# Sample keys turned by VectorE in 32x32 blocks and scored with 32x32-tile products

## The chip, the core and the metric

The kernel runs on one core of one Trainium2 chip. The metric is the device time of one execution in microseconds (us). Three runs of the kernel before took 1339.94, 1340.01 and 1341.91 us; the median is 1340.01 us.

## The reference, cut to what matters

The program is one inference step of a two-layer decoder: a short gated convolution layer and a native sparse attention (NSA) layer, each between two half-step SwiGLU networks, for 256 prompt tokens and 8 sequences of 4 new tokens ("samples"), model width 1024, 16 heads of 64 in 4 key/value groups, all in float32. The change is in the part of the NSA layer that attends from the sample tokens to their caches: a compressed branch, a selected branch (the 16 best of 32 blocks of 64 cached tokens) and a window branch (the last 512 cached tokens).

```python
s_s = jnp.einsum('bqkgd,bqkjld->bqkgjl', q, k_sel).astype(jnp.float32) * scale
s_s = jnp.where(m_s, s_s, NEG)
p_s = jax.nn.softmax(s_s.reshape(B, Tq, N_KV_HEADS, GROUP, n_sel * L_SEL), axis=-1)
o_s = jnp.einsum('bqkgjl,bqkjld->bqkgd', p_s.astype(q.dtype), v_sel)
...
s_w = jnp.einsum('bqkgd,bskd->bqkgs', q, kv_win[:, :, 0]).astype(jnp.float32) * scale
p_w = jax.nn.softmax(jnp.where(m_w, s_w, NEG), axis=-1)
o_w = jnp.einsum('bqkgs,bskd->bqkgd', p_w.astype(q.dtype), kv_win[:, :, 1])
```

The kernel does not gather blocks. It scores all 2048 cached tokens of a sequence and adds a large negative number to blocks that were not selected.

## The kernel before

The dense products (feed-forward networks, convolution, projections) run on TensorE (PE) as exact pairs: each weight is split into a high and a low part (`W.convert`: ScalarE copies, VectorE or GpSimd subtracts) and three products are added. They fill most of the execution and are not changed. Weights come through a ring of 4 buffers `raw` of 1 MB and a ring of 4 split pairs `whi`, `wlo`, in the order of a list; the SyncE queue (SP) issues their loads.

The NSA layer (`nsa`) first makes its projections: keys and values (6 blocks of 256 columns), gates, then the 8 query blocks `u`. A query block's prompt part goes to `qT`; its sample part goes to `Qbd`, a block-diagonal layout in which a sequence and a pair `pr` of key/value groups own 32 columns (2 groups x 4 tokens x 4 heads). Once all weights up to the attention have been loaded, `load_pages` starts to fill free `raw` buffers with cache pages; five more buffers, `page`, exist only from the attention on, since their pool (`att`) takes the room of a pool that the projections use (`tin`). A page is 512 tokens of one sequence, keys and values, 1 MB; each partition holds 4 tokens (index `s`). Window pages are loaded by SP, selected-branch pages by an indirect DMA on the GpSimd queue (POOL).

The attention then interleaves two streams by a hand-written order.

The samples: 4 pairs of sequences `i`, each with 5 chunks (window `w`, then 0 to 3) of one page for each of the two sequences, so 20 chunks `c`. For a chunk:

- `s_turn` (steps a and b, one for each sequence): PE transposes the page's keys, 8 transposes of 128x128 for each sequence; ACT copies 3 of the 4 resulting 128x512 PSUM tiles to SBUF, DVE the fourth, into the free split buffers.
- `s_scores` (step s): 4 products of K=128, 32 rows, 512 columns, in the four column tiles of the array, into one PSUM bank; DVE adds the mask, scales and takes the maximum in one instruction (line 1302), and ACT takes the exponential (line 1303).
- `s_turn_p` (step p): 4 transposes of the exponentials, copied by ACT to `PTs` (line 1316).
- `s_values` (step v): 16 products, 32 rows in the four column tiles; then the pages' buffers are free and `load_pages` issues the next loads.

Small steps for each pair (scores of compressed blocks and of new rows, ranking, weights of the branches, output) are hooked into the rounds.

The prompt: 8 units `u`, each of four items, `prompt_scores` twice (row half `kp` 0 and 1), `prompt_turn` (12 transposes and three copies to SBUF), `prompt_values`.

The order: `START = 'isabiiRiCS'` opens (i one prompt item, s the small scores, a and b the transposes, R the ranking, C a transpose for the prompt's compressed branch, S the scores of chunk 0). Then each round c runs `ROUND = 'abi0p1si2v'`: the transposes and scores of chunk c+1, the turn and values of chunk c, and 0.92 prompt items at each i as long as there are any, with a few kept for the last rounds. PE, DVE and ACT each take their instructions in the order in which the program puts them out; `soon` and `spend` keep an estimated clock, so that a step that hangs on another engine is put out later.

PSUM has 8 banks: in the attention 3 for scores (`mm`), 3 for transposes (`tr`), 2 for values (`acc`), each kind a ring.

Of the kernel before, what the change touches and what calls it, by code (L numbers as in the profile page):

```python
# [47 lines left out]
# the past blocks' compression beside the dense products: its share of the time, and what its loads take  # L48
# [11 lines left out]
KT_ACT, PT_ACT = (1, 2, 3), 1  # L60
# [84 lines left out]
def tile_step(ctx, tc, x_prompt, x_sample, state_conv, cache_cmp, cache_sel, cache_win, page_table,  # L145
# [33 lines left out]
    # ---- inputs wanted first  # L179
# [28 lines left out]
    # ---- constants  # L208
# [14 lines left out]
    # ---- the stream of weights  # L223
# [78 lines left out]
    # ---- the residual stream, transposed: [d, token]  # L302
# [54 lines left out]
    def begin(pg, pu):  # L357
        """The first products, each step as soon as its part of the input has been turned and split."""
# [66 lines left out]
    def products2(p0, p1, ah, al, late=2, between=None):  # L425
        """Two outputs at a phase's start: the inputs that come last are used last."""
# [182 lines left out]
    # ---- the last norm: turned as it comes, scaled when the tokens' factors are known  # L609
# [45 lines left out]
    # ---- the compressed branch's past blocks: they hang on the cache alone  # L655
# [8 lines left out]
    def indices():  # L664
        # a gathered row is two tokens of a block: partition (q, n) takes tokens 8 q + 2 i of block n
# [41 lines left out]
    def load_w1(pool):  # L707
        w = pool.tile([P, 16, P], F32, name="W1", bufs=1)
# [4 lines left out]
    def cmp_side(cw):  # L713
# [4 lines left out]
        # rows (q, d) and steps (i, l, h) of a block's token 8 q + 2 i + l and column 32 h + d  # L718
# [27 lines left out]
        # the first layer's share of the positions: a product with one column  # L746
# [53 lines left out]
    # ---- native sparse attention  # L800
    def nsa(at, v_next):
# [8 lines left out]
        def big(n, name):  # L810
            """A slot of the weights' split parts, free while attention runs."""
# [6 lines left out]
        W1 = load_w1(tin)  # L818

        # constants over rows r = (b2, pr, kp, t, g), tokens and blocks  # L820
# [48 lines left out]
        # a row's token is 4 * (b2 + 2 i) + t  # L869
# [7 lines left out]
        # new rows: of the row's own sequence, no later than its token  # L877
# [10 lines left out]
        # ---- projections  # L888
# [4 lines left out]
        nc.gpsimd.memset(Qbd, 0.0)  # L893
        R, V = {}, {}
# [7 lines left out]
        def rows(t, src, a):  # L902
            dst, dst_s, pb = outs[t]
            if a == 0:
                R[t] = T("Rk", [P, 2, 256])
                V[t // 2] = A(f"V{t}", [P, 2, 256]) if t else T("Rv", [P, 2, 256])
# [624 lines left out]
```

## Time and profile before

| | us |
|---|---|
| median of three runs | 1340.01 |
| span of the profiled execution (first to last instruction) | 1333.6 |
| attention stage in it, 918.65 to 1079.03 | 160.4 |
| PE busy in that stage | 153.4 |
| ACT busy in that stage | 110.5 |
| DVE busy in that stage | 94.2 |
| POOL busy in that stage | 49.5 |

The profile is of one execution. The own time of that execution is known only by its span; the runs' times also hold what lies around a span. In the profile's rows, PE is a matrix product, PEld a load of its stationary operand, DVE is VectorE, ACT ScalarE. A row of a group names the line, the engine, the operation, what is written and read, the shape, the count, then busy time and mean duration, then the idle time before with what ended it. A float32 product shows as two records. Products show the line of the helper that issues them (177, transposes 221), so their tiles tell them apart: `mm<-whi,Qbd` and `mm<-wlo,Qbd` are the sample scores, `tr<-ident,page` and `tr<-ident,raw` the key transposes, `acc<-page,PTs` and `acc<-raw,PTs` the sample values, `mm<-kT,qT` the prompt scores.

### The profile page before, as it was taken

The numbers are of one execution on the slowest core, as the hardware profiler recorded it, in microseconds if no ns is written. First come the engines' busy times: TensorE is split into PE (matmuls) and PEld (weight loads), VectorE is DVE, ScalarE is ACT, GpSimd is POOL, SyncE is SP. The second block draws the span as 40 slices with busy tenths as digits, with TensorE's granted clock in tenths as the row PEclk, the third lists the DMA queues.
The fourth block names the chain that finished last, engine by engine and source line by source line (L and its number), as shares of the span: only waits on it lengthen the run. The fifth ranks groups of instructions, "written<-read, shape, count | busy, mean of one in ns | idle before, by whom it ended". The sixth has DMA issues, their size and how long they took to land.

```text
span 1333.6 us, 26864 instructions
## 1 busy us (share of the span) xinstructions
PE 1309.6 (98%) x11009; PEld 1242.0 (93%) x11009; DVE 815.4 (61%) x1512; ACT 616.7 (46%) x1115; POOL 353.5 (27%) x356
## 2 busy tenths in 40 slices
PE   8999999999999999999999999999999999999997
PEld 8999999999999999999999999998776688999997
DVE  5675566677666555667655555666556456554553
ACT  5443444443454433345433445454766655443444
POOL 2331233243323222333321121303333123220211
PEclk9999999999999999999999999999999998999999
DMA  8767555756565575457656344765577964766432
GB/s 261 197 195 245 187 189 171 234 183 204 191 194 192 162 236 198 144 181 246 193 171 206 127 143 144 215 192 222 206 269 285 300 165 163 246 251 221 142 118 75
DMA packets 202893, 262.12 MB, mean 197 GB/s; under 512 B 14958, under 2 KB 188610, under 8 KB 197524
## 3 DMA queue, kind: packets, MB, share of 16 engines
q1 hardware_dynamic: 179792, 182.34, 43.5%
q0 software_dynamic: 14304, 75.61, 16.0%
q10 hardware_dynamic: 8676, 2.48, 1.0%
q8 instruction: 86, 1.41, 0.4%
q14 instruction: 35, 0.29, 0.1%
HBM read 257.38 MB, written 11.35 MB: 202 GB/s over the span
## 4 chain that ended last, share of the span: by engine, by line
PE 87%; DVE 6%; ACT 4%; issue 2%; POOL 1%; DMA 0%; ACTq 0%; SPq 0%; POOLq 0%; DVEq 0%
PE mm L177 74%; PE acc L177 8%; PE tr L221 4%; DVE wlo L117 2%; ACT whi L116 1%; DVE rt L739 1%; DMA rt<-in_x_prompt_dram 0%; ACT sq L332 0%; ACT wlo L1166 0%; ACT S L1166 0%; DVE xT L523 0%; ACT L527 0%; ACT whi L1280 0%; DVE xl L326 0%; POOL ue L542 0%
## 5 line engine op out<-in xcount | busy, mean ns | idle before, releaser
L177 PE MATMUL mm<-xh,whi 128*128 128x288 f32 x1832 | 548.5, 299 | 2.2 <-DVE xl L1215 0.9
L177 PE MATMUL mm<-xh,wlo 128*128 128x288 f32 x1832 | 544.1, 297 | 2.7 <-DVE wlo L117 1.7
L177 PE MATMUL mm<-xl,whi 128*128 128x288 f32 x1832 | 536.7, 293 | 1.1 <-DVE xl L326 1.1
L117 DVE TENSOR_TENSOR wlo<-raw,whi 128x1024 fp32r<-128x1024 f32 (+2 forms) x358 | 402.2, 1136 | 109.0 <-ACT whi L116 107.2
L116 ACT ACTIVATE whi<-raw 128x1024 fp32r<-128x1024 f32 (+2 forms) x365 | 343.1, 953 | 107.8 <-PE mm L177 90.7
L177 PEld LDWEIGHTS mm<-xh,whi 128*128 128x128 f32 x1832 | 344.8, 188 | 8.1 <-issue 3.9
L177 PEld LDWEIGHTS mm<-xl,whi 128*128 128x128 f32 x1832 | 349.1, 191 | 2.8 <-DVE xl L326 2.5
L177 PEld LDWEIGHTS mm<-xh,wlo 128*128 128x128 f32 x1832 | 344.2, 188 | 3.7 <-DVE wlo L117 2.4
L490 POOL TENSOR_TENSOR a<-s,t 128x288 f32<-128x288 f32 x88 | 111.9, 1271 | 445.8 <-DVE t L488 273.0
L177 PE MATMUL mm<-Ah,whi 128*128 128x288 f32 x768 | 229.4, 299 | 0.0
L177 PE MATMUL mm<-Ah,wlo 128*128 128x288 f32 x768 | 227.9, 297 | 0.7 <-DVE wlo L117 0.7
L177 PE MATMUL mm<-Al,whi 128*128 128x288 f32 x768 | 227.5, 296 | 0.0
L177 PEld LDWEIGHTS mm<-Ah,whi 128*128 128x128 f32 x768 | 145.2, 189 | 2.6 <-issue 1.9
L177 PEld LDWEIGHTS mm<-Ah,wlo 128*128 128x128 f32 x768 | 144.1, 188 | 1.4 <-DVE wlo L117 1.4
L177 PEld LDWEIGHTS mm<-Al,whi 128*128 128x128 f32 x768 | 144.4, 188 | 0.0
L486 ACT ACTIVATE s<-t 128x288 f32<-128x288 f32 x88 | 39.1, 445 | 172.4 <-DVE t L484 170.4
L733 POOL DMA_INDIRECT rc<-in_cache_cmp_kv_dram,idxc x64 | 70.8, 1107 | 134.2 <-DVE rt L739 117.0
L493 ACT ACTIVATE Ah<-a 128x288 fp32r<-128x288 f32 x88 | 39.2, 445 | 128.0 <-POOL a L490 127.7
L488 DVE TENSOR_TENSOR t<-mm,rB 128x288 f32<-128x288 f32 x88 | 39.9, 454 | 79.1 <-PE mm L177 79.1
L739 DVE STREAM_TRANSPOSE rt<-rc 128x1024 f32<-128x1024 f32 x64 | 78.3, 1233 | 9.2 <-PE acc L177 9.1
L494 DVE TENSOR_TENSOR Al<-a,Ah 128x288 fp32r<-128x288 f32 x88 | 40.0, 454 | 58.8 <-ACT Ah L493 58.8
L523 DVE SCALAR_TENSOR_TENSOR xT<-mm,xT 128x288 f32<-128x288 f32 x64 | 29.2, 456 | 71.2 <-PE mm L177 70.9
(348 smaller groups left out, 1249.3 us busy)
## 6 DMA issues: line engine op xcount, KB each, us to landing
raw<-in_w_ffb_gu_dram SPq DMA_DIRECT2D x44, 1024.0 KB
raw<-in_w_ffa_gu_dram SPq DMA_DIRECT2D x42, 1024.0 KB
raw<-in_w_ffa_down_dram SPq DMA_DIRECT2D x16, 768.0 KB
raw<-in_w_conv_in_dram SPq DMA_DIRECT2D x12, 1024.0 KB
raw<-in_w_ffb_down_dram SPq DMA_DIRECT2D x16, 768.0 KB
raw<-in_w_ffa_down_dram SPq DMA_DIRECT2D x16, 640.0 KB
raw<-in_w_ffb_down_dram SPq DMA_DIRECT2D x16, 640.0 KB
out_dram<-in_cache_win_kv_dram POOLq DMA_DIRECT2D x8, 1016.0 KB, 6.9
```

The costliest lines, as they stand in the source:

```text
L116: self.nc.scalar.activation(parts[0], v, AF.Copy)
L117: (lower or self.nc.vector).tensor_sub(parts[1], v, parts[0])
L177: nc.tensor.matmul(out, lhsT, rhs, start=start, stop=stop, skip_group_check=True)
L221: nc.tensor.transpose(out, in_, ident[:k, :k])
L486: nc.scalar.activation(s1, t1, AF.Silu)
L488: nc.vector.tensor_mul(t2, pu[:, :N], rB)
L490: nc.gpsimd.tensor_mul(a, s1, t2)
L493: nc.scalar.activation(Ah[:, f], a, AF.Copy)
L494: nc.vector.tensor_sub(Al[:, f], a, Ah[:, f])
L523: nc.vector.scalar_tensor_tensor(xT[:, d], py[:, :N], 0.5, xT[:, d], op0=OP.mult, op1=OP.add)
L733: nc.gpsimd.indirect_dma_start(out=tiles[i], out_offset=None, in_=rows_c, in_offset=bass.IndirectOffsetOnAxis(ap=idxc[:, i:i + 1], axis=0))
L739: nc.vector.transpose(turned[i], tiles.pop(i))
```

## The change

- `s_turn`: instead of 8 transposes on PE and two copies, one DVE instruction for each page transposes each 32x32 block of the keys in place (128 partitions x 4 x 256).
- A copy of the queries, `Qr`, repeats each 32-row piece of `Qbd` on all four 32-row groups, with zeros where the row of `Qbd` belongs to the other key/value group. `replicate` (step Q of START) makes it from 16 products with the identity and four copies, two on ACT, two on DVE. GpSimd clears it ahead.
- `s_scores`: 64 products of K=32, 32 rows, 128 columns, each in one of the 16 tiles of 32x32, four of them added up for one result; the four row groups write four different PSUM banks. The moving operand takes the four tokens of a partition as the inner index, 512 elements apart. The mask instruction reads the four banks at once, and the scores' order in SBUF becomes (token in page, s).
- `s_turn_p` reads the scores with four elements between neighbours.
- One PSUM tile `sc` of four banks holds the scores of samples and of the prompt; `tr` has two banks instead of three.
- `prompt_scores` handles one half of the queries at a time for both row halves `kp`, whose products follow each other in separate banks; all three copies of `prompt_turn` go to ACT.
- The five `page` buffers are allocated with the projections; two of them first hold `W1`, `XP` and two row buffers, and three are free for pages. Tiles that had room of their own (`S0`, `PB`, `PcT`) go to the split buffers and to `ss`.

```diff
-ATT = dict(mm=3, tr=3, acc=2)
+ATT = dict(tr=2, acc=2)
...
-START = 'isabiiRiCS'
+START = 'iQsabiiRiCS'
...
+        def page():
+            return at.tile([P, 2048], F32, name="page", bufs=PAGES)
+        W1 = load_w1(page())
+        XPR = page().rearrange("p (a x) -> p a x", a=4)
...
+        Qr = A("Qr", [P, NB * 2, 4, 32])
+        nc.gpsimd.memset(Qr, 0.0)
...
-        room = {"raw": 0, "page": 0}
+        room = {"raw": 0, "page": PAGES - 2}
...
             if W.loaded == W.stop:
-                room["raw"] = RAW - W.live - len(pages)
+                room["raw"] = RAW - W.live - sum(r == "raw" for r in rings.values())
                 load_pages()
+            else:
+                load_pages(True)
...
+        SC = banks["pool"].tile([P, 4, 512], F32, name="sc", bufs=1)
...
+        def replicate():
+            for c in range(4):
+                kp = c // 2
+                ps = accb()
+                cs = slice(c * 32, (c + 1) * 32)
+                for q4 in range(4):
+                    mm(ps[q4 * 32:(q4 + 1) * 32, :256], ident[cs, cs],
+                       Qbd[cs].rearrange("p b r x -> p (b r) x")[:, :, kp * 16:(kp + 1) * 16], True, True)
...
-        def prompt_scores(u, kp):
+        def prompt_scores(u, half):
...
+            b0 = 2 * (next(turns) % 2)
+            ps = [SC[:, b0], SC[:, b0 + 1]]
+            for br in range(2):
+                for kp in range(2):
+                    ks = slice(kp * 64, (kp + 1) * 64)
+                    mm(ps[kp][:, br * w:(br + 1) * w], qT[ks, u, qs], K[br + 1][ks, pr, :w], True, True)
...
         def s_turn(c, b2):
             i, j = chunks[c]
-            t = pages[i, j, b2]
-            KT[c, b2] = big(1024, ("whi", "wlo")[b2]).rearrange("p (a k) -> p a k", a=2)
-            for pr in range(2):
-                pt = trb()
-                for s in range(4):
-                    tr(pt[:, s * P:(s + 1) * P], t[:, s, pr * P:(pr + 1) * P])
...
+            k = pages[i, j, b2][:, :, :256]
+            nc.vector.transpose(k, k)
...
-            ps = mmb()
-            for q, b2, pr in groups():
-                mm(ps[q * 32:(q + 1) * 32], Qbd[:, 2 * i + b2, pr], KT[c, b2][:, pr], True, True)
...
+            for h in range(4):
+                kc = [slice(pr * P + h * 32, pr * P + (h + 1) * 32) for pr in range(2)]
+                for q4 in range(4):
+                    qs = slice(q4 * 32, (q4 + 1) * 32)
+                    for q, b2, pr in groups():
+                        mm(SC[q * 32:(q + 1) * 32, q4, :P], Qr[qs, 2 * (2 * i + b2) + pr, h],
+                           pages[i, j, b2][qs, :, kc[pr]].rearrange("p s x -> p x s"), h == 0, h == 3)
+            S = T("S", [P, P, 4], F32, 2)
```

More of the change, by code (lines that the diff above doesn't have):

```diff
@@ L59 @@
 HOOKS = ((-5, 1), (-3, 1), (3, 2), (4, 2), (5, 0), (5, 2))
-KT_ACT, PT_ACT = (1, 2, 3), 1
 EARLY = (2, 1)
@@ L928, in rows @@
                 nc.sync.dma_start(dst_s[0].rearrange("b t c k d -> (b t) (c k d)"), RS[pb:pb + NS])
-        XP = [T(f"XP{c}", [P, 16, KV, 8]) for c in range(2)]
+        XP = [XPR[:, c].rearrange("p (a k n) -> p a k n", k=KV, n=8) for c in range(2)]
         def cmp_prompt_in():
@@ L1035, in nsa, with load_pages @@
         pages, rings = {}, {}
-        room = {"raw": 0, "page": 0}
+        room = {"raw": 0, "page": PAGES - 2}
         done = []
-        def load_pages():
+        def load_pages(early=False):
             while len(pages) + len(done) < len(order):
-                ring = max(room, key=lambda r: room[r])
+                ring = "page" if early else max(room, key=lambda r: room[r])
                 if not room[ring]:
-                    return
+                    break
                 i, j, b2 = key = order[len(pages) + len(done)]
@@ L1046, in load_pages @@
                 room[ring] -= 1
-                t = raw.tile([P, 2048], F32, name="raw") if ring == "raw" else T("page", [P, 2048], F32, PAGES)
+                t = raw.tile([P, 2048], F32, name="raw") if ring == "raw" else page()
                 if j == "w":
@@ L1055, in load_pages @@
                 rings[key] = ring
-            W.stop, W.bufs = None, room["raw"]
-            W.load_ahead()
+            if not early and len(pages) + len(done) == len(order):
+                W.stop, W.bufs = None, room["raw"]
+                W.load_ahead()
         clock, due, ties = [0.0], [], count()
@@ L1148, in prompt_cmp2 @@
             nc.vector.tensor_copy(PcT, ps[:, :NP])
-        def prompt_scores(u, kp):
+        def prompt_scores(u, half):
             pr, g = divmod(u, 4)
-            if kp == 0:
-                units[u] = (big(4 * NP, ("whi", "wlo")[u % 2]).rearrange("p (j k) -> p j k", j=4), T("S0", [P, 4, P], F32, 2),
+            if half == 0:
+                units[u] = (big(4 * NP, ("whi", "wlo")[u % 2]).rearrange("p (j k) -> p j k", j=4), big(512, ("wlo", "whi")[u % 2]).rearrange("p (j k) -> p j k", j=4),
@@ L1169, in prompt_scores @@
+            if half:
                 soon(2.0, lambda: prompt_factor(u), ("u", u))
@@ L1437, in items @@
                 share[0] -= 1
-        room["page"] = PAGES
+        room["page"] += 2
         load_pages()
-        steps = dict(i=item, s=lambda: s_small(0), a=lambda: s_turn(0, 0), b=lambda: s_turn(0, 1), S=lambda: s_scores(0), R=lambda: s_rank(0), C=prompt_cmp2)
+        steps = dict(i=item, s=lambda: s_small(0), a=lambda: s_turn(0, 0), b=lambda: s_turn(0, 1), S=lambda: s_scores(0), R=lambda: s_rank(0), C=prompt_cmp2, Q=replicate)
         for step in START:
```

76 lines of the change are left out of this document (32 added, 44 removed).

## The prediction

> **What bounds the kernel now.** I read the page first, then the granted clock and busy times in stretches, then one round of the attention in the timeline, then the groups of instructions and the waits of that stage.
>
> ```profile
> span 1333.6 us, 26864 instructions
> PE 1309.6 (98%) x11009; PEld 1242.0 (93%) x11009; DVE 815.4 (61%) x1512; ACT 616.7 (46%) x1115; POOL 353.5 (27%) x356
> PE 87%; DVE 6%; ACT 4%; issue 2%; POOL 1%; DMA 0%; ACTq 0%; SPq 0%; POOLq 0%; DVEq 0%
> ```
>
> TensorE is the bound of the whole. The span is 1333.6 us, the median of the runs 1340.0, so 6.4 us lie around the span; I take it that this execution is like the median, work out a difference, and put it on 1340.0. The change touches only the attention stage (and some loads before it), so that stage decides. One round handles one chunk; the ACT copy of its turned scores (PTs, line 1316) marks it:
>
> ```profile
> 935.26 0.60 ACT L1316 ACTIVATE PTs<-tr 128x512 f32<-128x512 f32 x1
> 1024.83 0.62 ACT L1316 ACTIVATE PTs<-tr 128x512 f32<-128x512 f32 x1
> 1065.08 0.60 ACT L1316 ACTIVATE PTs<-tr 128x512 f32<-128x512 f32 x1 [0.25 <-PE tr L221]
> ```
>
> These are the 1st, 12th and 20th of the 20. They cut the stage, from the prompt's first scores to the output projection, into head, 11 rounds that also carry the prompt's items, 8 rounds almost without, and a drain (columns: stretch, its length, then busy time of PE, PEld, DVE, ACT and POOL, the clock granted, the DMA share and GB/s):
>
> ```profile
> 918.65:935.26 16.61, 15.65 (x124) 12.21 (x128) 13.34 (x69) 14.47 (x50) 5.29 (x4) 0.90 0.56 233
> 935.26:1024.83 89.57, 86.61 (x991) 62.21 (x993) 52.54 (x230) 62.02 (x196) 31.53 (x30) 1.00 0.66 244
> 1024.83:1065.08 40.25, 38.90 (x496) 27.96 (x491) 18.92 (x75) 24.11 (x58) 7.68 (x9) 1.00 0.98 324
> 1065.08:1079.03 13.95, 12.26 (x120) 8.82 (x120) 9.43 (x34) 9.88 (x28) 5.00 (x3) 1.00 0.79 146
> ```
>
> A mixed round lasts 89.57/11 = 8.14 us, a plain one 40.25/8 = 5.03. PE is busy 97% of both, DVE 59% and 47%. So PE sets the stage, and DVE has room: 37.0 us in the mixed rounds, 21.3 in the plain ones.
>
> **What leaves PE.** A round in full: its 16 key transposes, its four wide score products (two records each), its value products, and one item of prompt scores.
>
> ```profile
> 939.55 2.03 PE tr L221 x16
> 1017.81 0.96 PE mm L177 x8
> 1020.23 1.08 PE L177 MATMUL acc<-raw,PTs 128*32 128x128 f32 x32
> 1014.92 1.57 PE L177 MATMUL mm<-kT,qT 64*128 64x256 f32 x8
> ```
>
> The transposes go: 20 x 2.03 = 40.6 us of PE. The wide products go too: 20 x 0.96 = 19.2. Prompt scores now run the two row halves next to each other into separate banks; if they overlap, 8 items' worth of 1.57 is spared, 12.6 us at most, 0 at least; I take 10.
>
> **What comes to PE.** 64 products of 32x32 tiles a chunk, hence 128 records as each f32 product shows two. No row here has 32-row tiles side by side. The nearest rows bound it:
>
> ```profile
> 1017.50 0.31 PE L177 MATMUL acc<-kT,Qbd 128*32 128x32 f32 x16
> 1017.63 0.60 PE L177 MATMUL mm<-whi,Qbd 128*32 128x512 f32 x2
> 1018.06 0.60 PE L177 MATMUL mm<-whi,Qbd 128*32 128x512 f32 x2
> ```
>
> Sixteen records of four column tiles were put out between 1017.50 and 1017.63: 8.1 ns each. 128 x 8.1 = 1.04 us is the lower end, and some 0.2 us until the last one ends makes 1.25. The upper end is the value products, four column tiles abreast and the rows one after the other: 1.08/32 = 34 ns a record, 4.3 us a chunk. I take 1.25, nearer the lower end, because column tiles do run abreast here and the sixteen tiles are as independent. PE's work in the stage becomes 153.4 - 40.6 - 19.2 - 10 + 25 = 109 us: no longer the bound.
>
> [...] The new products read keys with 2 KB between neighbours, and the score transposes read S with 16 bytes between neighbours. No row before shows such a read; the price, if it binds, is worked out as a rival below. [...]
>
> Spreading the queries (16 products of 256 columns, four abreast) is 1.7 us of PE in the head: a wide product's second record starts 0.43 us after its first (1017.63, 1018.06), so 256 columns in two records take 0.43, four times. The head loses the transposes of two chunks, 4.1 us, against it.
>
> The score transposes' weight loads cost 0 more in my sum, and 0.56 us a round if they doubled (4 x 0.14); they lie beside DVE's work.
>
> **What comes to DVE, and what leaves it and ACT.**
>
> ```profile
> L739 DVE STREAM_TRANSPOSE rt<-rc x64: 1200/1236/1247, 75.7 to 745.8; 128x1024 f32<-128x1024 f32 x64
> L1282 DVE COPY whi<-tr 128x512 f32<-128x512 f32 x20 | 13.8, 688 | 8.5 <-PE tr L221 7.7 <-issue 0.8
> L1198 DVE COPY whi<-tr 128x512 f32<-128x512 f32 x4 | 2.8, 688 | 1.8 <-PE tr L221 1.8
> L1198 DVE COPY wlo<-tr 128x512 f32<-128x512 f32 x4 | 2.8, 688 | 1.6 <-PE tr L221 1.6
> L1280 ACT ACTIVATE wlo<-tr 128x512 f32<-128x512 f32 x40 | 22.2, 595 | 1.3 <-PE tr L221 1.3
> L1280 ACT ACTIVATE whi<-tr 128x512 f32<-128x512 f32 x20 | 11.8, 592 | 7.5 <-PE tr L221 7.3
> L1302 DVE CUSTOM_DVE_ANT_1 S<-mm,mk 128x512 f32<-128x512 f32 x16 | 11.0, 690 | 19.9 <-PE mm L177 19.9
> ```
>
> Two block transposes of 128x1024 a chunk: 2.47 us, 49.4 in all; in place and from four runs of 256 is not shown, and I price it the same. One copy of 0.69 a chunk goes (13.8), and the prompt's eight copies move to ACT (5.6). DVE in the stage: 94.2 + 49.4 - 19.4 + 0.8 (two of the four Qr copies at the 0.42 of a 128x256 group) = 125 us. ACT falls from 110.5 by 34.0 and gains 8 x 0.6 and 0.8: 82. DVE becomes the busiest engine.
>
> **The new wait.** Scores of samples and of the prompt now share one set of four banks (before: a ring of three). In a round DVE turns two pages, then PE can run the chunk's products, then DVE alone frees the banks (line 1302's 0.69). DVE's own queue stands still while PE works, 1.25 us a round, except for the small steps placed there (softmax factors, ranking); I take it half filled: 0.6. Behind DVE's waiting instruction stand the next chunk's transposes and the prompt's maxima, and PE waits for both. DVE's transposes also wait for the page, now at the head of DVE's queue rather than PE's:
>
> ```profile
> DMA to landing us min/median/max: 5.5/7.2/13.7
> ```
>
> Nine slots hold 4.5 chunks, so a page is asked for more than three rounds, 15 us, ahead: 0, at most a few us in the plain rounds where DMA already stands at 0.98.
>
> **The sum.** Mixed round on DVE: 52.54 busy - 11 x 0.69 - 5 x 0.69 (the prompt's copies) + 11 x 2.47 = 68.7, or 6.25 a round; + 0.6 = 6.85. Saved: 11 x (8.14 - 6.85) = 14.2 us. Plain round: (18.92 - 5.5 + 19.8)/8 = 4.15, + 0.8 (fewer small steps to fill with) = 4.95 against 5.03: saved 0.6. Head: 13.34 - 2.1 + 4.9 + 0.8 = 17 us of DVE in order plus its first waits, against 16.61: lost 2. Drain: one PE copy path against another, 0. Some rounds under the half clock (below): lost 3. Together -9.8: **1330 us**.
>
> **Edits at nothing.** The ring opening earlier: before, pages were issued from 900 on, and none held PE when the first transposes began.
>
> ```profile
> 900.03 1.02 POOL L1052 DMA_INDIRECT raw<-in_cache_sel_kv_dram,idxs  x1 [28.94 <-DMA out_dram<-RS]
> 915.93 0.94 POOL L1052 DMA_INDIRECT page<-in_cache_sel_kv_dram,idxs  x1 [0.30 <-issue]
> 920.89 3.14 PE L221 MATMUL tr<-ident,raw 128*128 128x128 f32 x16
> 867.76 0.25 POOL L699 TENSOR_TENSOR Hs<-Hs,Hx 128x32 f32<-128x32 f32 x1 [13.12 <-DVE lin L834]
> ```
>
> So earlier landing is hidden anyway; on SP and POOL the early issues pass only row outputs and the copy of Vc, which the first small values want some 30 us later. Without that cover it is 1 us an issue. Qr's clearing (128x2048 on POOL, about 2 us) falls into the 13 us that POOL stood idle before 867.76. Buffers that merely move (W1, XP, Rk, PcT, S0) cost nothing while their old readers are done.
>
> **Rivals.**
> (a) *DVE packed full.* If the waits vanish in small steps and overlap of successive instructions, the stage nears DVE's 125 us plus head and drain waits, say 135 of 160: 25 less, 1315. For: successive instructions on DVE start before the last one's shown end, so sums of durations are too high. Against: the single set of banks ties DVE to PE twice in rounds with prompt scores. Chance 0.13.
> (b) *Tile products dearer than what they replace* (slower). If rows run one after the other, a chunk takes 4.3 us: PE 109 + 20 x 3.05 = 170 us, bound again, plus the 7 of idle time that it has now: 177 against 160, 1356. If the strided reads halve the rate, a chunk takes about 2.3 us, 1.05 more in the chain between transposes and DVE's mask step, 20 x 1.05 = 21: 1351. [...] It decides from 1.25 + 9.8/20, about 1.75 us a chunk. For: no row shows either kind. Against: column tiles abreast. Chance 0.25.
> (c) *The clock falls.* Windows of 3.41 us:
>
> ```profile
> 916.51:919.92 3.41, 2.73 (x19) 2.42 (x18) 2.04 (x7) 0.00 (x0) 0.49 (x2) 1.00 1.00 404
> 919.92:923.33 3.41, 3.41 (x39) 3.12 (x38) 2.95 (x17) 2.91 (x8) 0.00 (x0) 0.50 1.02 430
> 930.16:933.57 3.41, 2.45 (x19) 1.77 (x17) 2.47 (x12) 3.41 (x13) 3.07 (x3) 1.00 0.01 2
> 1104.24:1107.65 3.41, 1.97 (x11) 1.25 (x9) 2.94 (x4) 3.15 (x8) 2.70 (x4) 1.00 0.01 2
> 1107.65:1111.07 3.42, 3.13 (x12) 2.24 (x10) 3.42 (x5) 3.21 (x6) 3.19 (x5) 0.50 0.00 0
> ```
>
> After windows at 80% and 58% PE busy the next was granted 0.50; one at 72% was not followed so. PE would be at 109/150 = 73%, in plain rounds near 55%. Half clock in 12 rounds beyond my 3 us, 1 us each: 1342. Chance 0.12.
> (d) *No gain*: overlap is as before, each saved copy's wait comes back as a bank wait, 1339 to 1341. Chance 0.08.
>
> **Chances and range.** My forecast has 0.42, with 1320 to 1337 as its own range. Less than 0.2% (2.7 us) from 1340 can't be told from no change. Faster: 0.40 + 0.13 = 0.53; same: 0.08 + 0.04 from (c) and my own upper edge = 0.12; slower: 0.25 + 0.10 = 0.35. The range takes in (a) and the half-rate end of (b): 1312 to 1354.
>
> **What would show it.** Sum right: the stage is about 150 us, DVE the busiest at 83% or so, mixed rounds at 6.9, plain ones at 5.0, transposes at 1.24 us each, a chunk's 128 records in 1.0 to 1.3 us. Wrong: records over 14 ns apart (b); clock under 0.9 across the stage (c); DVE waiting for PE more than 1.3 us a round; DVE waiting for pages; block transposes well over 1.24 us in place.

## The result, and the profile after

The changed kernel takes 1389.89 us (median of 4 runs, 1384.18 to 1392.76), the kernel before 1339.97 (4 runs, 1339.11 to 1341.91): ratio 1.0371, 95% interval 1.0353 to 1.0390. It is slower by 50 us; 1330 was predicted, with 1354 as the upper end. The profiled execution has a span of 1382.2 us, 48.6 more than the one before. From its page: span, the engines, the chain that ended last.

```profile
span 1382.2 us, 31038 instructions
PE 1318.1 (95%) x13121; PEld 1242.7 (90%) x13121; DVE 842.2 (61%) x1526; ACT 595.0 (43%) x1065; POOL 354.0 (26%) x357
PE 84%; DVE 8%; ACT 4%; issue 3%; POOL 1%; DMA 0%; ACTq 0%; SPq 0%; DVEq 0%; POOLq 0%
```

PE has 2112 product records and as many weight loads more. The attention stage, cut at the same five events as in the prediction (first prompt scores, 1st, 12th and 20th PTs copy, first product of the output projection); columns: stretch, length, busy time of PE, PEld, DVE, ACT, POOL, granted clock, DMA share, GB/s:

```profile
918.56:941.24 22.68, 14.62 (x244) 9.40 (x248) 16.93 (x72) 13.25 (x48) 3.06 (x2) 0.70 0.08 32
941.24:1052.26 111.02, 88.14 (x2132) 63.32 (x2130) 62.58 (x235) 50.54 (x167) 33.04 (x30) 0.94 0.52 192
1052.26:1114.33 62.07, 49.27 (x1345) 33.12 (x1347) 32.07 (x84) 14.09 (x36) 8.62 (x10) 0.92 0.70 227
1114.33:1128.57 14.24, 11.04 (x119) 7.30 (x119) 7.95 (x32) 10.89 (x30) 4.86 (x3) 1.00 0.66 130
```

The stage takes 210.0 us instead of 160.4, so it holds the whole loss: head +6.1, mixed rounds 10.09 us each instead of 8.14 (+21.5), plain ones 7.76 instead of 5.03 (+21.8), drain +0.3. PE was busy for 163 us where 109 were predicted; DVE for 119.5 where 125 were. No engine is full.

The timeline of PE shows one chunk's products whole, at full clock, and the groups of the stage show DVE's two steps (busy us, mean ns):

```profile
951.51 3.24 PE L176 MATMUL sc<-raw,Qr 32*32 32x128 f32 x128 [1.83 <-DVE mx L1195]
```
```profile
L1302 DVE STREAM_TRANSPOSE page<-page 128x1024 f32<-128x1024 f32 x21 | 25.5, 1227 | 0.0
L1302 DVE STREAM_TRANSPOSE raw<-raw 128x1024 f32<-128x1024 f32 x19 | 22.9, 1211 | 0.0
L1324 DVE CUSTOM_DVE_ANT_1 S<-sc,mk 128x512 f32<-128x512 f32 x16 | 11.1, 691 | 45.3 <-PE sc L176 45.3
```

A block transpose in place took 1.23 us on `page` and 1.21 on `raw`, close to the 1.24 that were taken. This chunk's products cost 3.24 us, not 1.25: 25 ns a record, beyond the 14 that the prediction named as the sign of its rival (b), and DVE waits 45.3 us for the products of 16 chunks. In the mixed rounds, chunks at full clock and without a stop take 2.90 to 3.35 us. At 3.24 a chunk, 20 chunks are 20 x 2 = 40 us above the sum (measured from first product to last, stops and waits inside included, the 20 take 74.7 us in all, where the sum had 25), and the first theory was that the stride of the keys makes them slow. But some chunks show something else. The chain of waits, 980 to 990 us (start, length, what):

```profile
980.51 2.79 PE sc L176 x94
983.30 3.40 issue
986.70 0.69 PE sc L176 x5
```

PE stands still for 3.40 us in the middle of a chunk and waits for nothing that the profile shows ("issue"). The DMA queues name a candidate. Columns: packets, MB, share; the whole execution before, then after, then the attention stage alone before, then after:

```profile
q8 instruction: 86, 1.41, 0.4%
```
```profile
q8 instruction: 103, 1.69, 0.5%
```
```profile
q8 instruction: 13, 0.21, 0.5%
```
```profile
q8 instruction: 30, 0.49, 0.9%
```

1.41 MB in 86 packets is 16.4 KB each. PE and PEld have 2 x 11009 records before and 2 x 13121 after: divided by the packets that is 256 and 255. So by the count this queue brings PE's instructions, 256 to a packet; such a packet's worth is called a block here. A chunk's tile products are 128 products and 128 weight loads, one whole block, used up in 3.2 us; before, a block lasted 160.4/13 = 12.3 us. The queues during the stop above, 983.2 to 986.8 us:

```profile
q0 software_dynamic: 88, 0.59, 39.8%
q8 instruction: 1, 0.02, 1.7%
```

One block of instructions arrives there, between 88 packets of the queue that brings the selected pages.

PE's waits in the stage (in total, times, longest one; those for the exponentials and for keys just turned, and the smaller ones, are left out):

```profile
PE sc L176 <- DVE mx L1195: 14.2, 9, 3.0
PE sc L176 <- issue: 6.2, 2, 3.4
PE sc L176 <- DVE nb L1324: 4.2, 5, 1.0
PE acc L176 <- issue: 4.0, 3, 1.7
PE tr L220 <- ACT wlo L1227: 3.2, 4, 1.5
PE tr L176 <- issue: 2.0, 1, 2.0
PE tr L220 <- ACT whi L1227: 1.6, 2, 1.4
```

12.2 us are issue; 18.4 are waits for DVE's maxima and mask steps, which have to empty the score banks.

Where the issue stops stand tells what they are. Counted from the start of the trace over all of PE's instructions in it (products, weight loads, semaphore instructions), five of the six (3.40, 1.68, 2.85, 0.81 and 1.47 us, together 10.2) come at numbers that leave 193 or 194 on division by 256: whole blocks lie between them. The sixth, 2.0 us in the head, stands elsewhere and is in every version with the change. The packets of q8 fit: one starts after each such edge, and by the stops its block is wanted at the next. Before the change it starts a median 1.2 us after the edge (at most 3.6) and the next edge is some 12 us away, and no stop stands at an edge; after the change it starts a median 2.3 us after it (at most 4.6) and takes about 1 us more, and at the five stops PE goes on 1.2 to 1.7 us after the packet has ended.

### The profile page after: what moved, and what is told of

The parts are those of the page before. It is cut to its first block, busy times and chain, and to the rows that moved or that the text cites. A ratio compares the mean times of both kernels' runs of the same rounds, so it can differ in the third digit from the quotient of the medians.

```text
span 1382.2 us, 31038 instructions
## 1 busy us (share of the span) xinstructions
PE 1318.1 (95%) x13121; PEld 1242.7 (90%) x13121; DVE 842.2 (61%) x1526; ACT 595.0 (43%) x1065; POOL 354.0 (26%) x357
## 4 chain that ended last, share of the span: by engine, by line
PE 84%; DVE 8%; ACT 4%; issue 3%; POOL 1%; DMA 0%; ACTq 0%; SPq 0%; DVEq 0%; POOLq 0%
PE mm L176 69%; PE acc L176 7%; PE sc L176 5%; DVE wlo L116 2%; PE tr L220 2%; ACT whi L115 1%; DVE raw L1302 1%; DVE page L1302 1%; DVE rt L738 1%; DVE S L1324 1%; DVE whi L1195 0%; DVE wlo L1195 0%; ACT sq L331 0%; DMA rt<-in_x_prompt_dram 0%; ACT S L1327 0%
```

## The experiments

All times are medians of four runs or more; in brackets the ratio to the kernel before on the same chip with its 95% interval. The letters A to I are theories of what costs the time; each is spelled out in the expectation that was recorded ahead of its run.

### The stride (theory A), the small tiles (B), the banks (C)

The keys are read as runs of 32 neighbours, and the columns are put in their places in PSUM instead; the scores' layout in SBUF becomes (s, token):

```diff
-mm(SC[q * 32:(q + 1) * 32, q4, :P], Qr[...], pages[i, j, b2][qs, :, kc[pr]].rearrange("p s x -> p x s"), h == 0, h == 3)
+mm(SC[q * 32:(q + 1) * 32, q4, :P].rearrange("p (x s) -> p s x", s=4), Qr[...], pages[i, j, b2][qs, :, kc[pr]], h == 0, h == 3)
-S = T("S", [P, P, 4], F32, 2)
+S = T("S", [P, 4, P], F32, 2)
```

> The changed kernel with both strided reads taken out: the tile products read their keys in runs of 32 neighbouring elements and put the columns in their places in PSUM instead, and the scores lie in SBUF so that their transposes read neighbours. Theory A (the stride in the moving operand slows the tile products): a chunk's 128 records fall from about 3.1 us to 1.1 to 1.4 us, 20 x 1.8 = 36 us less, about 1350 us or lower. Theory B (it is the 16 small tiles themselves: issue, weight loads, row groups): records stay at 3 us a chunk and only the score transposes' 20 x 0.15 = 3 us go, 1384 to 1388 us. Theory C (the single set of four banks that ties DVE to PE): as B, within 3 us of it.

1389.53 us (1.0383, 1.0366 to 1.0400): no gain. The second run has the first half of the edit alone:

> Only the keys' read is made of neighbours (columns spread in PSUM), the score transposes still read every fourth element. Theory A: chunk 1.1 to 1.4 us, the same time as with both taken out but for the transposes' 3 us: about 1353 us. Theory B or C: 1385 to 1391 us.

1388.35 us (1.0370, 1.0353 to 1.0387). The third has the second half:

> Only the scores' layout in SBUF is changed, so that their transposes read neighbours; the keys are still read with 2 KB between neighbours. If the strided transposes cost only what their rows show (0.75 against 0.60 to 0.66 us for four): 2 to 3 us less, 1387 us. If the strided read costs more by the wait behind it (ACT's copy and the value products): up to 10 us less, 1380 us. Theories A, B and C expect the tile products unchanged at about 3.1 us a chunk.

1393.11 us (1.0401, 1.0384 to 1.0419). And the loops over row groups and column tiles exchanged:

```diff
-for q4 in range(4):
-    for q, b2, pr in groups():
+for q, b2, pr in groups():
+    for q4 in range(4):
```

> The 64 tile products of a chunk in another order: four row groups of a column tile one after the other instead of four column tiles of a row group. Theory A (strided reads, each tile limited by its own operand stream): no difference, 1385 to 1392 us, chunk 3.0 to 3.3 us. Theory B in its form 'order and issue' (a product waits for the tile before it in the queue): chunk changes by over 0.3 us, the time by over 6 us either way.

1387.57 us (1.0363, 1.0346 to 1.0381). By the times alone A had fallen. The timelines of PE say otherwise; the same chunk with both reads contiguous, then with the exchanged loops:

```profile
951.46 1.90 PE L176 MATMUL sc<-raw,Qr 32*32 32x128 f32 x128 [1.92 <-DVE mx L1195]
```
```profile
953.65 2.79 PE L176 MATMUL sc<-raw,Qr 32*32 32x128 f32 x128 [1.83 <-DVE mx L1195]
```

Contiguous reads take 1.34 us off a chunk at full clock, 27 us if all 20 ran so, and the time does not fall by any of it. Something else holds the stage. What the stage of the contiguous version shows (columns as above):

```profile
918.57:1130.12 211.55, 158.50 (x3830) 112.71 (x3831) 125.37 (x421) 87.22 (x279) 49.31 (x45) 0.78 0.53 180
```

It is as long as before the edit, PE is busy for 4.6 us less, and the mean clock is 0.78. As the granted clock stands at 1.00 or 0.50 throughout the traces before and after, (1 - 0.78) x 2 x 211.6 = 93 us ran at half clock; after the change it was 210.0 us at 0.91, 38 us; before the change 16.61 us at 0.90 and the rest at 1.00, 3 us. At half clock the gain of a chunk is 0.03 us. One chunk with both reads contiguous, then one with the exchanged loops, each at half clock (columns as above):

```profile
934.28:937.10 2.82, 2.81 (x128) 2.12 (x128) 0.63 (x4) 1.54 (x8) 2.32 (x2) 0.50 0.04 9
936.39:939.24 2.85, 2.85 (x128) 2.12 (x128) 0.64 (x4) 1.55 (x8) 2.34 (x2) 0.50 0.04 9
```

The contiguous chunk has gone from 1.90 to 2.82 us, the strided one from 2.79 to 2.85. And the stops at block edges have grown from 10.2 to 16.2 us. The 20 chunks, from first product to last, took 62.0 us instead of 74.7.

The third run missed even its small gain. The groups of its stage show why:

```profile
L1324 DVE CUSTOM_DVE_ANT_1 S<-sc,mk 128x512 f32<-128x512 f32 x16 | 16.8, 1048 | 46.7 <-PE sc L176 46.7
```

DVE's mask step, which now writes every 128th element, takes 1.05 us instead of 0.69. The stride went from PE's weight loads to DVE's output: 20 x 0.36 = 7 us of DVE, in every run below with this layout.

### The chain of the round (D) and the clock (E)

Block transposes a round ahead of the mask step that they stood behind:

```diff
 for step in START:
     steps[step]()
+for b2 in range(2):
+    s_turn(1, b2)
...
-                    else:
-                        s_turn(n, int(step == "b"))
+                elif n + 1 < NC:
+                    s_turn(n + 1, int(step == "b"))
```

> The changed kernel, its strided reads as they are, but DVE turns the pages of chunk c+2 ahead of the mask step of chunk c+1 (one round earlier), so that the next chunk's tile products need not wait for mask step, block transposes and hand-over one after the other. Theory D (the loop of the round is a chain: block transposes 2.47 us, tile products about 3.1 us, mask step 0.8 us, in one row; nothing overlaps them): plain rounds fall from 7.8 us to about 5 us, mixed ones from 10.1 to 8 or less, together 8 x 2.5 + 11 x 2 = 42 us at most, 1347 to 1365 us. Theory E (the half clock sets the time, whatever the order): less than 12 us less, 1378 to 1390 us. Theory B (PE itself is full with the tile products): no change, 1385 to 1392 us.

1384.00 us (1.0333, 1.0316 to 1.0350), 5 us less than the changed kernel by the ratios, plain rounds at 7.85 us. The same with contiguous reads:

> As the run before it, with the keys and the scores read as neighbours too (chunk's products 1.90 us at full clock). Theory D: 20 x 1.2 us less PE work than that run, part of it behind DVE: 1325 to 1350 us. Theory E: the freed PE time brings the half clock in again, as in the runs with the contiguous reads alone: no less than the run with the strided reads, 1350 to 1390 us.

1384.77 us (1.0325, 1.0303 to 1.0348). D's 25 to 40 us are not there. Products of no use, with contiguous reads:

```diff
+for _ in range(3):
+    mm(o[:, 256:512], ident, kT[2][:, 0, :256], True, True)
```

> The kernel with both reads contiguous (1389.5 us), with three more products of 128x128 by 256 columns after each chunk's value products, into PSUM columns that nothing reads: 20 x about 1.3 us of work that is added and of no use. Theory E (the clock falls to half because PE idles, and that takes back the 24 us that contiguous reads gain): the extra work raises the granted clock, and the time falls by 8 to 20 us, to 1370 to 1381 us. Theory D (the chain, the clock being a symptom): the extra work lies in PE's waits at best, 1386 to 1410 us.

1403.94 us (1.0480, 1.0463 to 1.0498), and the last two edits together:

> Block transposes a round ahead, contiguous reads, and the three useless products a chunk. If the half clock still holds that order back: faster than without the useless products, by 5 to 15 us. If not: slower by up to 20 x 1.3 = 26 us, as PE's waits are shorter there.

1395.69 us (1.0416, 1.0395 to 1.0438). The useless products, in the groups of the stage:

```profile
L176 PE MATMUL acc<-kT,ident 128*128 128x256 f32 x120 | 34.8, 430 | 0.1
```

34.8 us of work lengthened the time by some 13 us (1.0383 to 1.0480); the mean clock of the execution rose from 0.963 to 0.977, so some half clock went. But no gain came from it: E as the sole cause falls. What did grow from the changed kernel (12.2 us) to the version with both edits is issue, 21.9 us. Its waits of PE:

```profile
PE acc L176 <- issue: 11.0, 4, 4.0
PE sc L176 <- issue: 8.5, 11, 3.8
PE tr L176 <- issue: 2.0, 1, 2.0
PE tr L220 <- issue: 0.4, 1, 0.4
```

Where PE could have gone faster, it stood longer for nothing that the profile shows; 17.5 of the 21.9 us stand at block edges, and in all eleven versions with 64 products a chunk, here and below, every issue stop over 0.5 us does, but for the one in the head. Hence theory F.

### The supply of instructions (F)

On that version, half as many products of twice the columns. It uses half of the query rows, so what it adds up are no scores; the runs below with half the pages, half the columns or half the products leave out work as well, and serve for their time alone.

```diff
-for h in range(4):
-    kc = [slice(pr * P + h * 32, pr * P + (h + 1) * 32) for pr in range(2)]
+for h in range(2):
+    kc = [slice(pr * P + h * 64, pr * P + (h + 1) * 64) for pr in range(2)]
...
-mm(SC[q * 32:(q + 1) * 32, q4, :P]...
+mm(SC[q * 32:(q + 1) * 32, q4, :256]...
```

> Block transposes a round ahead, contiguous reads (the version of 1384.8 us), but a chunk's scores in 32 products of 256 columns in place of 64 of 128: as many columns streamed, half as many instructions (it uses half of the query rows, twice the columns; what it adds up are no scores). Theory F (TensorE runs out of instructions: the profile's instruction queue brings blocks of 16 KB, each 256 PE records, and a chunk's tile products alone use up one block in 2 to 3 us): the idle stretches put down to 'issue' (22 us in the attention) fall below 6 us, the chunks that took 3 to 4 us take 1.9, and the time falls by 20 us or more, to 1335 to 1365 us. Theory E (the half clock): as much streaming and as much idle time, so within 8 us of 1384.8. Theory B in its form 'number of products': the chunk's 1.90 us fall to 1.0 to 1.3 us.

1361.58 us (1.0180, 1.0163 to 1.0197): 1.0325 less 1.0180 is some 19 us (the raw times, 23 apart, are from two chips that ran the kernel before in 1340.3 and 1336.9). Of issue only the 2.0 us in the head are left. And half the pages, with all instructions:

```diff
-order = [(i, j, b2) for i, j in chunks for b2 in range(2)]
+order = [(i, j, b2) for i, j in chunks for b2 in range(1)]
...
-pages[i, j, b2]
+pages[i, j, 0]
```

> Block transposes a round ahead, contiguous reads, with all instructions of the engines but with half of the cache pages loaded: both sequences of a pair read the first one's page. Theory F with contention (the instruction blocks come late because they stand behind the pages' packets, DMA share 0.9 to 1.0): 'issue' falls from 22 us to below 8, time 1350 to 1372 us. Theory F without contention (a block takes its 2 to 4 us anyway): 'issue' stays at 15 to 22 us, time within 6 us of 1384.8. Theory G (PE and DVE wait for pages): time falls, and waits for pages, not 'issue', are what shrinks.

1364.48 us (1.0206, 1.0187 to 1.0224): some 16 us less by the ratios, with issue at 9.3 us, of which 7.2 stand at block edges:

```profile
PE sc L176 <- issue: 4.6, 4, 2.2
PE acc L176 <- issue: 2.7, 3, 2.3
PE tr L176 <- issue: 2.0, 1, 2.0
```

The packets of q8 start a median 1.0 us after an edge here, 2.7 with all pages. That is what the contention form of F says, though issue did not fall below the 8 us that it named.

In the versions with the transposes a round ahead DVE wants the pages earlier, and waits for them. Its waits with all products, then with half of them:

```profile
DVE raw L1302 <- DMA raw<-in_cache_sel_kv_dram,idxs: 5.5, 2, 2.9
```

```profile
DVE raw L1302 <- DMA raw<-in_cache_sel_kv_dram,idxs: 14.4, 4, 5.3
```

This can be why going ahead by a round gains nothing once PE is fast; it was not tried by itself. So the next runs go back to the order of the changed kernel. First its strided reads, with half the products:

> The changed kernel, its strided reads and its order as they are, but a chunk's scores in 32 products of 256 columns in place of 64 of 128: as many columns, half the instructions (half of the query rows are used, and what it adds up are no scores). Theory F (instruction supply): 15 to 25 us less than 1389.9, 1365 to 1375 us, chunk 2.9 to 3.2 us throughout, stretches of 'issue' under 6 us. Theory A (stride) beside F: this one stays 10 to 24 us above the same with contiguous reads. Theory A alone: no change, 1385 to 1392 us.

1364.71 us (1.0189, 1.0172 to 1.0206). Its stage, and all of its issue waits:

```profile
918.60:1106.88 188.28, 151.46 (x2550) 87.31 (x2550) 120.17 (x421) 87.66 (x279) 49.58 (x45) 0.92 0.59 200
```
```profile
PE tr L176 <- issue: 2.0, 1, 2.0
PE tr L220 <- issue: 0.4, 1, 0.4
```

No stop at a block edge is left, and the mean clock is 0.92 where it was 0.91: between these two runs the clock is not what changed.

Then contiguous reads:

> The same with contiguous reads, order of the changed kernel: 32 products of 256 columns a chunk (no scores, as in the run before it). If the stride matters once instructions do not bind (A beside F): 1345 to 1360 us. If not: within 5 us of the strided one. If the transposes a round ahead mattered in the earlier run of this kind (1361.6): over 8 us above that.

1358.26 us (1.0136, 1.0119 to 1.0153); issue is 2.5 us, none of it at an edge. Half the pages on top:

> The run before it with half of the cache pages loaded as well (both sequences of a pair read the first one's page, 32 products of 256 columns). If instruction supply and page transfers are the whole loss: 1335 to 1345 us. If the ring of score banks, the waits of the round and the half clock hold a part: 1345 to 1360 us, and waits of PE for DVE's maxima (about 14 us) stay. If pages never mattered but for the instructions: the same as the run before it within 4 us.

1361.58 us (1.0165, 1.0148 to 1.0182). PE waits 6.3 us there for block transposes of `page` buffers, 2.2 in the run before it, which can hide a small gain. And the counterpart, all 64 products of half the columns:

```diff
-... .rearrange("p (x s) -> p s x", s=4), Qr[...], pages[i, j, b2][qs, :, kc[pr]], ...
+... .rearrange("p (x s) -> p s x", s=4)[:, :2], Qr[...], pages[i, j, b2][qs, :2, kc[pr]], ...
```

> Contiguous reads, order of the changed kernel, all 64 products of a chunk, but of 64 columns instead of 128 (two of the four tokens of a partition are left out of the scores): all instructions, half the streaming. Theory F: the time stays within 8 us of the 1389.5 with all columns, 'issue' is 20 us or more. Theory B or A (streaming): 15 us less or more than that, 1360 to 1375 us.

1386.61 us (1.0361, 1.0339 to 1.0383). Waits of PE in this last one:

```profile
PE sc L176 <- issue: 12.4, 7, 5.5
PE acc L176 <- issue: 7.4, 3, 3.0
PE tr L176 <- issue: 4.0, 2, 2.0
```

The cross is clear. Half the instructions: 25.2 us less with strided reads, 31.3 with contiguous ones. Half the columns: 2.9 less, within the intervals, and issue rises from 18.6 to 23.8 us. Half the pages: some 16 us less as long as all instructions are there (of which at most the 5.5 us above were waits for pages as such), and nothing once the instructions are halved (3.3 us more; this pair has the order of the changed kernel, the other the transposes a round ahead). So in these runs the pages cost time mainly by making the instruction blocks late (a median 2.7 us after an edge with all pages, 1.0 with half). The contiguous pair is less pure than the strided one: with half the instructions its clock was 0.84 instead of 0.78, with half the columns 0.73. The stride costs 6.4 us (1364.7 against 1358.3) once instructions do not bind, less than the 10 to 24 expected; 7 us more of DVE stand against that.

### What is left

Two parts of the change were put into the kernel before. The prompt's scores by halves, with the ring of three score banks that it has:

```diff
-for S, qs, w, m, j0 in (...):
-    ps = mmb()
+S, qs, w, m, j0 = (...)[half]
+ps = [mmb(), mmb()]
+for br in range(2):
+    for kp in range(2):
+        mm(ps[kp][:, br * w:(br + 1) * w], qT[ks, u, qs], K[br + 1][ks, pr, :w], True, True)
```

> The kernel before with one part of the change alone: the prompt's scores by halves of the queries, the products of both row halves after each other in two banks of the ring of three. The prediction's term of 10 us: PE sets the end of the stage before, so 1330 us (1328 to 1333). If the row halves do not overlap, or if two banks at once make PE wait for the ring: 1338 to 1345 us.

1336.86 us against 1336.94 (1.0002, 0.9993 to 1.0012). The prompt scores of PE in the stage, before and in this run (both widths in one row):

```profile
L177 PE MATMUL mm<-kT,qT 64*128 64x256 f32 (+1 forms) x128 | 24.9, 339 | 0.5 <-DVE pc L1094 0.5
L177 PE MATMUL mm<-kT,qT 64*128 64x128 f32 (+1 forms) x128 | 15.4, 350 | 1.7 <-DVE mx L1167 1.2 <-DVE pc L1094 0.5
```

The row halves do overlap: 9.5 us of PE are spared. None of it reaches the end of the stage, which takes 162.6 us; PE's waits for the copies of turned tiles have grown from 4.6 to 9.2 us. And with `ATT = dict(mm=4, tr=2, acc=2)`:

> The same with four banks for scores and two for transposes. If the ring of three held the version before it back: faster than that by 1 to 5 us. If the transposes want three banks: slower than that, up to 1345 us.

1355.46 us (1.0138, 1.0122 to 1.0155). Its waits of PE:

```profile
PE tr L221 <- ACT whi L1282: 10.4, 10, 2.0
PE tr L221 <- DVE whi L1284: 7.6, 15, 1.4
```

Two transpose banks cost that kernel 18.6 us: the copies of the turned keys are close behind PE, although PE was busy for 97% of the rounds before.

At last, half of each chunk's products left out, which at full clock is the prediction's price of a chunk or less:

```diff
-for h in range(4):
+for h in range(2):
...
-..., h == 0, h == 3)
+..., h == 0, h == 1)
```

> The changed kernel's order with contiguous reads, and half of a chunk's products left out: 32 of 128 columns (the scores are summed over half of the query rows only). Half the instructions and half the streaming, about 1.0 us a chunk, the price that the prediction took or less. If the rest of the prediction's sum holds (DVE's 125 us, 0.6 us of waits a round): 1325 to 1335 us, mixed rounds 6.9 us, plain ones 5.0. If the round's waits hold the rest (PE for DVE's maxima, the transposes' ring of two, half clock): 1350 to 1358 us, mixed rounds 8.3 to 8.8.

1354.67 us (1.0116, 1.0099 to 1.0133). And with columns apart:

```diff
-b0 = 2 * (next(turns) % 2)
-ps = [SC[:, b0], SC[:, b0 + 1]]
+x0 = (256, P)[half]
...
-mm(ps[kp][:, br * w:(br + 1) * w], qT[ks, u, qs], ...
+mm(SC[:, 2 * kp + br, x0:x0 + w], qT[ks, u, qs], ...
```

> The run before it, and samples and prompt in columns of their own in the four score banks (samples 0 to 127, the prompt's two halves of the queries 128 to 255 and 256 to 511), so that no product has to wait until another stream's scores have been read. Theory H (the shared set of banks ties PE to DVE): the 14 to 17 us of PE waiting for DVE's maxima fall below 5 us, and the time by 8 to 16 us. Theory I (the waits are only where PE happens to stand, as DVE or the copies of the transposes set the round): the waits move to another place and the time stays within 4 us.

1353.88 us (1.0116, 1.0095 to 1.0137). Its waits of PE:

```profile
PE sc L176 <- DVE mx L1194: 15.7, 9, 3.5
```

This run settles nothing: the wait that it should take away is still there (the samples' products still begin when the prompt's maxima end), so neither H nor I was tried. The stage of the run before it:

```profile
919.92:1098.71 178.79, 137.07 (x2551) 93.27 (x2551) 126.36 (x421) 86.34 (x279) 49.34 (x45) 0.79 0.63 210
```

Stage by stage, cut at the same five events in each trace (us):

| | head | mixed round | plain round | drain | stage |
|---|---|---|---|---|---|
| before | 16.6 | 8.14 | 5.03 | 14.0 | 160.4 |
| forecast, with 3 us of half clock | 18.6 | 6.85 | 4.95 | 14.0 | 150.6 |
| after | 22.7 | 10.09 | 7.76 | 14.2 | 210.0 |
| contiguous | 23.3 | 9.95 | 8.07 | 14.2 | 211.6 |
| half the products, twice the columns, strided | 22.6 | 9.15 | 6.35 | 14.2 | 188.3 |
| the same, contiguous | 24.3 | 8.75 | 6.02 | 14.2 | 183.0 |
| half the products | 23.3 | 8.72 | 5.66 | 14.2 | 178.8 |
| before, prompt by halves | 19.1 | 8.16 | 5.00 | 13.8 | 162.6 |
| the same, two transpose banks | 21.1 | 9.45 | 5.53 | 13.7 | 183.0 |

## Why the prediction was wrong

The sign was wrong: 1330 us was forecast, 10 us less than before, and 1389.9 was measured. The failing steps of the sum:

*The price of a chunk, 1.25 us.* It was taken from how far apart sixteen small records start, with their streaming hidden. The 1.90 us above is one of four contiguous versions. The other three, each at full clock (each of the four figures stands, within 0.04 us, on four or five chunks of its run):

```profile
953.80 1.49 PE L176 MATMUL sc<-raw,Qr 32*32 32x256 f32 x64 [1.92 <-DVE mx L1195]
```
```profile
951.32 1.47 PE L176 MATMUL sc<-raw,Qr 32*32 32x64 f32 x128 [1.92 <-DVE mx L1195]
```
```profile
953.56 1.07 PE L176 MATMUL sc<-raw,Qr 32*32 32x128 f32 x64 [1.92 <-DVE mx L1195]
```

With the 1.90 above, halving the records takes 0.41 or 0.40 off, halving the columns 0.43 or 0.42. So, as an estimate from these four that takes the costs of records and columns as proportional, putting out 128 records costs about 0.82 us (6.4 ns each) and streaming about 0.85, and the two add up, with 0.23 left over; the prediction had counted the first, at 1.04, and 0.2. By the same estimate the strided read makes streaming 3.24 - 0.82 - 0.23 = 2.19 us, 2.6 times as much (with the loops exchanged 1.74, twice). That is the strided form of the prediction's rival (b), which put the chunk at 2.3 us; the half rate in it was the author's estimate, shown by no row before. In time, the price of streaming is worth little as long as instructions come late: nothing for the stride, 2.9 us for half the columns. Once instructions do not bind, the stride is worth 6.4 us.

*A term that no part of the sum had: the supply of instructions.* The prediction counted the durations of 128 records a chunk, and not that 256 instructions have to be brought in for them, while pages are being loaded. By time this is the largest step: halving the instructions gives 25 to 31 us in the cross above. About 20 x 0.41 = 8 of that is the time to put the records out. The stops at block edges, of which products of twice the columns leave none, were 10.2 us with strided reads and 16.2 with contiguous ones. The 7 us that remain of each pair are not taken apart here. Neither the forecast nor a rival had the term, so (b) too ended at 1351 to 1356, far from 1390.

*Prompt scores, 10 us.* The work did fall as forecast (24.9 us before, 16.5 in the changed kernel, 15.4 in the kernel before with this part alone), the time did not: 0.9993 to 1.0012 in the kernel before. "PE sets the stage" was read from 97% busy; of the work spared, half came back as longer waits for the copies of transposed tiles, the rest as several small waits. The same holds for the transposes' ring of two, at which the prediction set no price: 18.6 us in the kernel before. In the changed kernel, with no key transposes, PE waits for ACT's copies only 4.8 us (3.2 and 1.6).

*The round, 6.85 and 4.95 us.* With a chunk at 1.07 us at full clock, less than the 1.25 taken, rounds take 8.72 and 5.66 and the kernel 1354.7, not 1330. That version's dearer mask step adds 7 us of work to DVE, and stops at block edges are still 3.4 us of it. DVE's work was summed rightly, but it is not packed: in a mixed round block transposes, prompt maxima, tile products and mask step follow each other, and PE waits 14.2 us for maxima and 4.2 for mask steps in the changed kernel; 0.6 us a round was meant for all of it. That the shared banks are the reason is not shown, since the run that was to show it left the waits in place. So the cause of these 25 us stays open in part: waits for DVE and the half clock are both in it.

*The clock, 3 us.* 38 us of the stage ran at half clock, 13.6 of them in the head ((1 - 0.70) x 2 x 22.68), which lost 6.1 us; 2.0 of these are the issue stop that is at no block edge. In the version with half the products it was (1 - 0.79) x 2 x 178.8 = 75 us. What this costs by itself is open: the version with more clock had more work too. The rival on the clock also took PE in plain rounds for 55% busy; its own rows give (38.90 - 8 x (2.03 + 0.96 - 1.25))/39.6 = 63%.

Right were the block transposes' 1.24 us (1.21 to 1.23 measured), DVE's sum (119.5 against 125), the PE work of the prompt's scores, the head's direction, and that pages, as pages, hold nobody up in this order: no wait of DVE or PE for a page stands in the waits of the stage after. The score transposes' strided weight loads cost a little (four take 0.75 us against 0.60 to 0.66), and moving the stride to DVE's output costs more (0.36 us a chunk).

No version here beats the kernel before. Chunks of twice the tokens would give each product 256 columns and halve the instructions in earnest; that was not tried, and the run that imitates it, at 1358.3, says that it would still lose.

## What to carry to other kernels

Count instructions as well as their durations: where a step puts out hundreds of short ones within a few microseconds while large transfers run, look at the instruction queue's packets and at "issue" in the chain, count whether the stops lie whole blocks of instructions apart, and halve the count at equal streaming to see what it costs. A fix that makes one step faster and leaves the time where it was is no proof that the step was cheap: with other limits in force, contiguous reads brought the same chunk at full clock from 3.24 to 1.90 us, and took nothing off the time. And a busy share of 97% does not say that work taken from that engine shortens the stage; the next wait may stand close behind it.

## What the runs showed of the hardware that was not expected

By the counts of this case PE's instructions came in packets of 16.4 KB, 256 instructions each. In the stage after the change one came every 7.0 us on the mean (210.0/30) and a chunk's products used up a whole block in 3.2 us; at block edges, beside page loads, PE stood still for up to 3.40 us (up to 5.5 with half the columns). By the estimate above, from chunks of 1.90, 1.49, 1.47 and 1.07 us, products of 32x32 tiles cost 6.4 ns a record plus their streaming, in sum rather than the larger of both, and with 2 KB between neighbours of the moving operand a chunk's streaming took 1.74 to 2.19 us instead of 0.85 at full clock, 2.0 to 2.6 times as much; at half clock a strided chunk took 2.85 us (2.79 at full clock, loops exchanged) and a contiguous one 2.82 (1.90). The granted clock was 0.91 over the stage with strided reads and 0.78 with contiguous ones, at about the same length of stage (210.0 and 211.6 us) and with 163.1 and 158.5 us of PE busy.
